# Two more pairs of groups as Strassen pairs in a hybrid decoder layer: the first gate groups and the first output groups

## The chip, the cores and the metric

The kernel runs on one core of one Trainium2 chip. The metric is the device time of one execution in microseconds (us), the median of several runs; lower is better. The profile adds one execution that was recorded by the hardware profiler.

## The reference

One layer of a decoder trunk on 256 tokens with a model width of 2048, all in float32:

```python
h = rmsnorm(x, norm_mix_g)
u = h @ w_in                       # 2048 x 12288
c_g, b_g, xa, za, q, fl, iv, og, ga, gb = split(u)    # eight of 1024 columns, ga and gb of 2048
ya = b_g * causal_dwconv3(c_g * xa, conv_w) * silu(za)
o  = hgrn2_chunked(silu(q), kk(fl), iv, log_f(fl))    # gated linear recurrence, 8 heads of 128
yb = (o / rms(o) * hg_norm_g) * silu(og)
m  = sigmoid(ga) * (ya @ w_a_out) + sigmoid(gb) * (yb @ w_b_out)
x  = x + m @ w_o
x  = x + sigmoid(rmsnorm(x, ple_norm_g) @ w_ple_gate) * (p @ w_ple_proj)
return rmsnorm(x, final_norm_g)
```

## The kernel before

**Groups and steps.** The work is a list of *groups*. A group is a product of the 256 tokens (two row tiles of 128, `t` = 0 and 1) with 512 columns of a weight matrix. It runs over the rows of the weights in *steps* of 256 rows, each a tile of 128 x 1024 (two row tiles of 512 columns). The order is written out: four groups `PP`; for j = 0 and 1 the groups f, q, iv, og, c, xa, za, b; then for j = 0 to 3 the gates ga and gb and the groups A and B (the products with `w_a` and `w_b`, four steps each); then four output groups O with `w_o`, and the groups of `w_pg`. TensorE goes through the steps in this order.

**Precision.** Every float32 operand is split into a rounded high part and the rest, so that a product takes three matmuls: hi x hi, hi x lo, lo x hi. `split(pos)` makes the two parts of a step's weights: an ACTIVATE on ScalarE writes `whi` (L161), a subtraction on VectorE writes `wlo` (L162). A plain step is 2 x 2 x 3 = 12 matmuls of 512 columns.

**Pairs.** Some neighbouring groups run as a *pair* with a program such as

```python
GATES = ("S", 0), (0, 2), ("S", 1), (1, 2), ("S", 4), (0, 6), ("S", 5), (1, 6)
```

An item `(u, c)` stands for two plain steps of group u, from chunk c on; a chunk is 256 rows. An item `("S", c)` is a Strassen unit: chunk c of both groups at once, as a 2 x 2 x 2 block product with seven block products in place of eight, so 21 matmuls where two plain steps take 24. It has four steps, or parts. Its weights have to be combined: `combine_weights` (L176, L179, L180) does three subtractions and additions on VectorE behind the split of part 0; part 1 is a half split of 512 columns (`t2`), parts 2 and 3 are splits of the combined weights. The left operand needs sums of its blocks too: `forms` computes them on VectorE (L761 to L765), and splits them like everything else (on VectorE L769). For h the forms come from a second reading of xT (`forms_of_x`). A pair holds all eight PSUM banks: four of tag g, one for each row tile and group, and four of tag s. `sums` adds the banks up at its end (L810). Before, the pairs are QV and VG (parts of j = 0 and 1), GG for the gates of j = 1, 2 and 3, and GP among the groups of `w_pg`.

**Epilogues.** What follows a group is a generator (`ep_...`), advanced by a yield at every step, so that its instructions stand in the engines' queues between the splits. `turned` turns a tile round: four DMAs to DRAM, one back, and a transpose on VectorE (L332). `ep_bb` multiplies and adds the two branches into a quarter of m, turns it, and splits it into `mh` and `ml` (L889, L890).

**Queues and buffers.** Splits run ahead of their step by `LEAD` = 3 and more. A split needs a buffer: four pairs in pool `wp`, and in some stretches one or two more (`MORE`). The buffer is free when the step that used it before is done. Weights come through three `raw` buffers by SyncE's (SP) DMA queue, which also carries the turning and all else. Each engine takes its instructions in the order of its own queue, which is fixed when the kernel is built.

**Pools.** Two changes of memory pools touch the change: `second_part` closes `tmp1` (with the recurrence's tiles) and opens `m` and `tmp2`, once, after ga of j = 0; `third_part` closes `tmp2` and `branch` and opens `tmp3`, with two steps of the first O group left. Both let all running epilogues finish first.

Of the kernel before, what the change touches and what calls it, by code (L numbers as in the profile page):

```python
# [15 lines left out]
P = 128  # L16
# [25 lines left out]
GATES = ("S", 0), (0, 2), ("S", 1), (1, 2), ("S", 4), (0, 6), ("S", 5), (1, 6)  # L42
INNER = (0, 4), ("S", 0), (0, 6), ("S", 1), (2, 3), ("S", 2), (1, 4), (1, 6)
FRONT = (0, 2), (0, 4), (0, 6), ("S", 0), (1, 2), ("S", 1), (1, 4), (1, 6)
LATE = (0, 4), ("S", 0), (0, 6), ("S", 1), (2, 3), ("S", 2), (1, 4), (1, 6)


# [6 lines left out]
def hybrid_kernel(ctx, tc, xT, x, pT, prm, gfin, masks, w_in, w_a, w_b, w_o, w_pg, w_pp, out):  # L54
# [28 lines left out]
    def nm(s):  # L83
        uid[0] += 1
        return f"{s}_{uid[0]}"
# [17 lines left out]
    half = {}  # L103

    def load(pos):
        w, g, c = stream[pos]
        if unit_of[pos] not in loaded:
            raw = wp.tile([P, 2, 2 * CW], F32, tag="raw", bufs=3, name=nm("raw"))
            loaded[unit_of[pos]] = raw
            if joint[pos]:  # L110
                nc.sync.dma_start(out=raw[:, 0, :], in_=w[g, :, c, :])
                for i in range(2):
                    nc.sync.dma_start(
                        out=raw[:, 1, i * CW : (i + 1) * CW], in_=w[g + 1, :, c, (1 - i) * CW : (2 - i) * CW]
                    )
            elif across[pos]:
                for i in range(2):
                    nc.sync.dma_start(out=raw[:, i, :], in_=w[g + i, :, c, :])
            elif FIRST <= pos < FIRST + 20:
                for i in range(2):  # L120
                    nc.sync.dma_start(out=raw[:, i, :], in_=w[g, :, c + i, :])
            elif pos >= FIRST:
                with ExitStack() as order:
                    if groups[steps[pos][0]][0] == "O":
                        order.enter_context(tc.issue_after(state["sent"]))
                    nc.sync.dma_start(out=raw, in_=w[g, :, c : c + 2, :])
        return loaded[unit_of[pos]]

    def load_first(pos, queues):
# [8 lines left out]
    def split(pos, c0=0, c1=2 * CW):  # L138
        part = part_of[pos]
        src = load(pos)[:, part % 2, :]  # L140
        if joint[pos]:

            src = load(pos)[:, part == 3, :]
            if part == 1:
                src, c1 = half[unit_of[pos]], CW

        pool, n = (pools["late"], 6) if (pos - state.get("late", len(steps))) % 10 < 6 and "late" in state else (wp, 4)
        places = [(pool, n, tag) for tag in ("whi", "wlo")]
        n = len(MORE[more(pos)])
        if pos % (4 + n) < n:  # L150
            places = [(pools[name], 1 + (tag == "X"), tag) for name, tag in MORE[more(pos)][pos % (4 + n)]]
        if pos not in parts:
            parts[pos] = tuple(
                pool.tile([P, 2 * CW], F32R, tag=tag, bufs=n, name=nm("w" + x)) for (pool, n, tag), x in zip(places, ("hi", "lo"))
            )
        hi, lo = parts[pos]
        s = slice(c0, c1)
        with ExitStack() as order:
            for i in (*(state["splits"] if more(pos) == "inner" else ()), *(state["before"].pop() if state.get("before") else ())):
                order.enter_context(tc.issue_after(i))  # L160
            a = nc.scalar.activation(out=hi[:, s], in_=src[:, s], func=AF.Copy)  # L161
            v = nc.vector.tensor_tensor(  # L162
                out=lo[:, s], in0=src[:, s], in1=hi[:, s].bitcast(F32), op=ALU.subtract
            )
        state["splits"] = (a.ins, v.ins)
        if joint[pos] and part == 0:
            combine_weights(pos)

    def combine_weights(pos):

        b = load(pos).rearrange("p i (k c) -> p (i k) c", k=2)
        pool, tag, n = ("tmp2", "t2", 2) if pos in gates else ("tmp3", "t2", 1)
        if more(pos) == "inner":
            pool, tag, n = "tmp1", ("both", "aoff")[unit_of[pos] // 2 % 2], 1
        t2 = half[unit_of[pos]] = pools[pool].tile([P, CW], F32, tag=tag, bufs=n, name=nm("t2"))
        nc.vector.tensor_tensor(  # L176
            out=b[:, 0:4:3, :], in0=b[:, 0:3:2, :], in1=b[:, 3:4, :].to_broadcast([P, 2, CW]), op=ALU.subtract
        )
        nc.vector.tensor_tensor(out=t2, in0=b[:, 2, :], in1=b[:, 0, :], op=ALU.add)  # L179
        nc.vector.tensor_tensor(out=b[:, 1, :], in0=b[:, 1, :], in1=t2, op=ALU.subtract)  # L180
# [3 lines left out]
    for n, (kind, j) in enumerate(IN_ORDER):  # L184
        if (kind, j) in (("q", 0), ("iv", 1)):
            groups.append(("VG", j, w_in, n, "hT", INNER) if j else ("QV", j, w_in, n, "hT", FRONT))
        elif (kind, j) in (("iv", 0), ("og", 1)):
            continue
        elif j == 0 or kind not in ("ga", "gb"):
            groups.append((kind, j, w_in, n, "hT"))  # L190
        elif kind == "ga":
            groups.append(("GG", j, w_in, n, "hT", GATES))
        if kind == "gb":
            groups.append(("A", j, w_a, j, "yaT"))
            groups.append(("B", j, w_b, j, "ybT"))
    groups += [("O", j, w_o, j, "mT") for j in range(4)]
    groups += [("PG", 0, w_pg, 0, "x1T"), ("GP", 1, w_pg, 1, "x1T", LATE), ("PG", 3, w_pg, 3, "x1T")]
    steps = []
    active, done = [], 0
# [8 lines left out]
    for gi, (kind, j, w, g, op, *program) in enumerate(groups):  # L208
# [4 lines left out]
        for n, (u, c) in enumerate(program[0]):  # L213
# [10 lines left out]
    LEAD = 3  # L224
    MORE = {
        None: (), "gates": ((("tmp2", "whi"), ("tmp2", "wlo")),),
        "inner": (
            (("tmp1", "X"), ("tmp1", "X")), (("tmp1", "a"), ("tmp1", "y")),
        ),
    }  # L230
    of_kind = lambda *kinds: [pos for pos, (gi, c) in enumerate(steps) if groups[gi][0] in kinds]
    gates, late = of_kind("GG"), of_kind("PG")[0]
    gates = range(gates[0] - 12, gates[-1] + 9)
    inner = [of_kind(kind) for kind in ("QV", "VG")]
    inner = range(inner[0][0] - 3, inner[0][-1] + 1), range(inner[1][0] - 6, inner[1][-1] + 1)

    def more(pos):

        return "gates" if pos in gates else "inner" if any(pos in at for at in inner) else None

    TOKENS, NORM, FORMS, MASKS = 10, 13, 5, 30
    FIRST = 6
# [552 lines left out]
    def forms_of_x(joined, made):  # L795

        for n in range(0, len(joined), 2):
# [8 lines left out]
            yield from forms("hT", made(n), r, chunks)  # L806
            yield

    def add(out, x, y):
        nc.vector.tensor_tensor(out=out, in0=x, in1=y, op=ALU.add)  # L810

# [45 lines left out]
    def ep_inner(j, e, left):  # L857
# [307 lines left out]
    def third_part():  # L1165
# [7 lines left out]
        xs, state["more"] = whole[:, : NT * D].rearrange("p (t d) -> p t d", t=NT), whole[:, NT * D : NT * D + 1]  # L1173
        state["x"], state["whole"] = xs, whole
        residual(0)
        state["ss2"] = sc(8, "ss2", 1)
        state["ss3"] = sc(12, "ss3", 1)
        nc.gpsimd.memset(state["ss3"].rearrange("p (t j) -> p t j", t=NT)[:, :, 5:6], EPS)
# [11 lines left out]
    def advance():  # L1190
        for e in list(active):
            step(e)
# [78 lines left out]
    for pos, (gi, c) in enumerate(steps[:last_group]):  # L1271
# [43 lines left out]
            step(active[-1])  # L1315
        if pos == MASKS:
            nc.sync.dma_start(out=mask_t, in_=masks)
        if program:
            program = program[0]
            if c == (0, 0):  # L1320
                total = products_of(program)
                left, banks = dict(total), {}
            if c == (min(n for n, (u, _) in enumerate(program) if u == "S"), 0):
# [42 lines left out]
        if c == nch - 1:  # L1366
            if kind == "f" and j == 0:

                waiting = psum
            if kind == "ga" and j == 0:  # L1370
                finish()
                second_part()
                active.append(forms_of_x(sorted(c for u, c in GATES if u == "S"), lambda n: form_tiles(pools["tmp2"], f"Sx{n}")))
                step(active[-1])
            if kind == "O" and j == 0:
                state["x1T"] = operand(big, "x", KT)
            if kind == "f" and j == 0:
                continue
            active.append(epilogues[kind](j, psum))
# [100 lines left out]
```

## Time and profile before

| | us |
|---|---|
| median of 3 runs | 811.68 (811.56 to 811.70) |
| the profiled execution | 810.99 |
| its span, first to last instruction | 809.2 |
| TensorE (PE) busy | 799.4 |
| VectorE (DVE) busy | 657.4 |
| ScalarE (ACT) busy | 474.6 |

The page's row of tenths shows each engine's busy share in 40 slices of the span; a group's row gives line, engine, operation, output and inputs, shape and count, then busy time and the mean of one in ns, then the idle time of the engine before them and what ended it. A window's row gives busy times of PE, PEld (weight load), DVE, ACT and POOL, then the granted clock, the DMA share and GB/s. In the timeline a row has start and length in us. The stages named in the text: the ga and gb groups of j = 0 run from 375.00 to 418.52 us, the first GG pair from 440.28 to 481.08, the O groups from 627.96 on.

### The profile page before, as it was taken

To read this page: it belongs to the slowest core of one execution; us is meant where nothing else is said; L and a number is where in the kernel's file an instruction comes from. 1 tells how busy PE (TensorE), PEld (TensorE's weight loads), DVE (VectorE), ACT (ScalarE), POOL (GpSimd) and SP (SyncE) were. 2 spreads that over 40 slices of the span, in tenths; PEclk is the share of its full clock that TensorE was granted. 3 is DMA by queue.
4 is the path that set the end of the run, shared out by engine and by line. 5 is a ranking of instruction groups with operands and counts; after the bars stand their busy time and mean duration, and the time that the engine had idled before them with its cause. 6 is when DMAs were issued, how large, how long until landed. Compare 5 with 4: busy or idle time off the path is not lost.

```text
span 809.2 us, 11053 instructions
## 1 busy us (share of the span) xinstructions
PE 799.4 (99%) x4183; PEld 665.1 (82%) x4184; DVE 657.4 (81%) x786; ACT 474.6 (59%) x627; POOL 92.1 (11%) x74
## 2 busy tenths in 40 slices
PE   9999999999999999999999999999999999999995
PEld 7888888888888888888888888888888888888885
DVE  5979897967889987967868998998996657679894
ACT  6967565555664765555664564565564456665662
POOL 0000145300000144300001001000100000001032
PEclk9999999999999999999999999999999999999998
DMA  9898856647677654656774774674766687887532
GB/s 342 301 338 312 274 183 207 222 159 247 238 256 228 240 196 170 228 188 228 266 240 151 240 274 146 226 271 150 254 250 217 217 300 262 288 300 272 205 133 105
DMA packets 47862, 188.60 MB, mean 233 GB/s; under 512 B 5440, under 2 KB 14912, under 8 KB 33088
## 3 DMA queue, kind: packets, MB, share of 16 engines
q1 hardware_dynamic: 47664, 187.62, 66.9%
q8 instruction: 33, 0.54, 0.3%
q10 hardware_dynamic: 144, 0.26, 0.1%
q14 instruction: 21, 0.17, 0.1%
HBM read 174.23 MB, written 13.63 MB: 232 GB/s over the span
## 4 chain that ended last, share of the span: by engine, by line
PE 91%; DVE 5%; issue 2%; ACT 1%; DMA 1%; POOL 0%; ACTq 0%; POOLq 0%; DVEq 0%
PE g L1210 62%; PE g L1232 20%; PE s L1232 6%; DVE wlo L162 2%; DMA raw<-in_w_pg 1%; PE s L1210 1%; PE s L482 1%; DVE t L971 1%; PE s L1085 1%; DVE raw L176 0%; DVE t L810 0%; DVE xs L972 0%; DVE t L989 0%; PE s L615 0%; PE s L638 0%
## 5 line engine op out<-in xcount | busy, mean ns | idle before, releaser
L162 DVE TENSOR_TENSOR wlo<-raw,whi 128x1024 fp32r<-128x1024 f32 (+1 forms) x315 | 387.6, 1250 | 119.5 <-ACT whi L161 118.3
L161 ACT ACTIVATE whi<-raw 128x1024 fp32r<-128x1024 f32 (+1 forms) x315 | 323.0, 1048 | 216.0 <-PE g L1210 157.1
L1210 PE MATMUL g<-whi,xh 128*128 128x512 f32 (+1 forms) x528 | 202.3, 384 | 0.0
L1210 PE MATMUL g<-wlo,xh 128*128 128x512 f32 (+1 forms) x528 | 202.1, 383 | 0.0
L1210 PE MATMUL g<-whi,xl 128*128 128x512 f32 (+1 forms) x528 | 201.9, 383 | 0.0
L1210 PEld LDWEIGHTS g<-whi,xl 128*128 128x128 f32 x528 | 99.2, 188 | 19.4
L1210 PEld LDWEIGHTS g<-whi,xh 128*128 128x128 f32 x528 | 99.3, 188 | 19.3
L1210 PEld LDWEIGHTS g<-wlo,xh 128*128 128x128 f32 x528 | 99.3, 188 | 19.2
L1232 PE MATMUL g<-whi,xl 128*128 128x512 f32 x264 | 102.7, 389 | 0.0
L1232 PE MATMUL g<-wlo,xh 128*128 128x512 f32 x264 | 102.7, 389 | 0.0
L1232 PE MATMUL g<-whi,xh 128*128 128x512 f32 x264 | 102.4, 389 | 0.0
L1232 PEld LDWEIGHTS g<-wlo,xh 128*128 128x128 f32 x264 | 49.6, 188 | 10.3
L1232 PEld LDWEIGHTS g<-whi,xl 128*128 128x128 f32 x264 | 49.6, 188 | 10.3
L1232 PEld LDWEIGHTS g<-whi,xh 128*128 128x128 f32 x264 | 49.6, 188 | 10.3
L161 ACT ACTIVATE whi<-t 128x512 fp32r<-128x512 f32 x20 | 12.6, 632 | 70.3 <-DVE t L179 70.3
L1210 PE MATMUL g<-whi,mh 128*128 128x512 f32 x128 | 49.8, 389 | 0.0
L1210 PE MATMUL g<-wlo,mh 128*128 128x512 f32 x128 | 49.8, 389 | 0.0
L1210 PE MATMUL g<-whi,ml 128*128 128x512 f32 x128 | 49.6, 389 | 0.0
L883 POOL TENSOR_TENSOR t<-ga,gb 128x512 f32<-128x512 f32 x6 | 10.6, 1786 | 190.5 <-issue 118.1
L1210 PEld LDWEIGHTS g<-wlo,mh 128*128 128x128 f32 x128 | 24.0, 188 | 5.0
L1210 PEld LDWEIGHTS g<-whi,mh 128*128 128x128 f32 x128 | 24.0, 188 | 5.0
L1210 PEld LDWEIGHTS g<-whi,ml 128*128 128x128 f32 x128 | 24.0, 188 | 4.9
(287 smaller groups left out, 1003.9 us busy)
## 6 DMA issues: line engine op xcount, KB each, us to landing
raw<-in_w_in SPq DMA_DIRECT2D x70, 1024.0 KB, 4.9
raw<-in_w_in SPq DMA_DIRECT2D x35, 512.0 KB, 5.1
raw<-in_w_o SPq DMA_DIRECT2D x16, 1024.0 KB, 5.9
raw<-in_w_pg SPq DMA_DIRECT2D x12, 1024.0 KB, 5.4
turn<-t SPq DMA_DIRECT2D x72, 128.0 KB, 2.6
t<-turn SPq DMA_DIRECT2D x18, 512.0 KB, 4.9
raw<-in_w_in SPq DMA_DIRECT2D x34, 256.0 KB, 4.7
raw<-in_w_a SPq DMA_DIRECT2D x8, 1024.0 KB, 5.2
```

Source lines behind the costliest of these rows:

```text
L161: a = nc.scalar.activation(out=hi[:, s], in_=src[:, s], func=AF.Copy)
L162: v = nc.vector.tensor_tensor(out=lo[:, s], in0=src[:, s], in1=hi[:, s].bitcast(F32), op=ALU.subtract)
L482: nc.tensor.matmul(heads(bk)[r, h, c if at is None else slice(at, at + 32)], key(h)[:, r], query(h)[:, c], start=True, stop=True, tile_pos ...
L883: (nc.vector if j == 3 else nc.gpsimd).tensor_tensor(out=spread(m, t), in0=blocks(ga[:, s]), in1=blocks(gb[:, s]), op=ALU.add)
L971: nc.vector.tensor_tensor(out=gt[:, s], in0=gt[:, s], in1=pw[:, s], op=ALU.mult)
L1085: nc.tensor.matmul(wb[:m, :n], *ones, start=True, stop=True)
L1210: nc.tensor.matmul(psum, a, b, start=first and n == 0, stop=last and n == 2)
L1232: nc.tensor.matmul(banks[name], x, y[:, s], start=k == total[name] and i == 0, stop=k == 1 and i == 2)
```

## The change

The gate groups ga and gb of j = 0 become a pair G0 with the program `GATES`, and the first two O groups a pair OO with a new program `OUT`. Each has four Strassen units. G0's forms of h are made early, in tiles of `tmp1`, by a further reading of xT, and made again in `tmp2` for the later pairs. OO needs forms of m: `ep_bb` stores the first two quarters of m, turned, in DRAM, and `forms_of_m` reads them back during A of j = 3. The change of pools and the start of the pair's epilogue move to G0's last unit (`opening`) and to the last unit of OO. Buffers for splits are added in G0 (from `tmp1`) and in OO (from `yaT`), and in the stretches `tied` each split is held in order behind the one before. The residual of x is loaded for two output groups at once.

```diff
+OUT = ("S", 0), (0, 4), ("S", 1), (1, 4), ("S", 2), (0, 6), ("S", 3), (1, 6)
...
-            for i in (*(state["splits"] if more(pos) == "inner" else ()), *(state["before"].pop() if state.get("before") else ())):
+            for i in (*(state["splits"] if more(pos) == "inner" or any(pos in at for at in tied) else ()), *(state["before"].pop() if state.get("before") else ())):
...
-        elif j == 0 or kind not in ("ga", "gb"):
+        elif kind not in ("ga", "gb"):
             groups.append((kind, j, w_in, n, "hT"))
         elif kind == "ga":
-            groups.append(("GG", j, w_in, n, "hT", GATES))
+            groups.append(("GG" if j else "G0", j, w_in, n, "hT", GATES))
...
-    groups += [("O", j, w_o, j, "mT") for j in range(4)]
+    groups += [("OO", 0, w_o, 0, "mT", OUT), ("O", 2, w_o, 2, "mT"), ("O", 3, w_o, 3, "mT")]
...
+        "last": ((("tmp2", "whi"), ("tmp2", "wlo")), (("branch", "yaTh"), ("branch", "yaTl"))),
+        "first": ((("tmp1", "a"), ("tmp1", "y")), (("tmp1", "b"), ("tmp1", "v"))),
...
-    gates = range(gates[0] - 12, gates[-1] + 9)
+    opening = of_kind("G0")[0] + max(n for n, (u, c) in enumerate(GATES) if u == "S") * 3 + 3
+    g0 = range(of_kind("G0")[0], opening + 1)
+    tied = [range(opening - 21, opening + 12), range(of_kind("OO")[0] - 2, of_kind("OO")[0] + 28)]
+    gates = range(opening + 5, of_kind("OO")[0] + 2)
+    last = range(gates[-1] + 1, gates[-1] + 21)
...
+    def forms_of_m():
+        for j in range(2):
+            raw = t4()
+            nc.sync.dma_start(out=raw, in_=state["m", j])
+            yield
+            yield
+            yield
+            r = raw.rearrange("p (u k t) -> p u k t", u=2, k=2)
+            yield from forms("mT", form_tiles(pools["tmp2"], f"Sx{2 * j}"), r, (2 * j, 2 * j + 1))
...
+    def ep_out(j, e, left):
+        def then(q, g):
+            after = ep_o(j + q, [g[:, A], g[:, B]])
+            next(after)
+            active.append(after)
+        yield from sums(e, left, lambda: (t4(), t4()), then)
...
+        if j < 2:
+            d = state["m", j] = dram.tile([P, 1024], F32, tag="m", bufs=2, name=nm("m"))
+            yield
+            yield
+            nc.sync.dma_start(out=d, in_=m)
...
+        if pos == g0[0] - 9:
+            homes = lambda n: lambda: tuple(
+                pools["tmp1"].tile([P, 1024], F32R, tag=tag, bufs=1 + (tag == "X"), name=nm("form"))
+                for tag in (("kT", "qT") if n else ("X", "X"))
+            )
+            active.append(forms_of_x(sorted(c for u, c in GATES if u == "S"), homes))
+            step(active[-1])
...
+            if kind == "OO" and c == (6, 3):
+                finish()
+                third_part()
+                state["x1T"] = operand(big, "x", KT)
+                active.append(ep_out(j, banks, left))
+                step(active[-1])
+            if pos == opening:
+                finish()
+                second_part()
+                active.append(forms_of_x(sorted(c for u, c in GATES if u == "S"), lambda n: form_tiles(pools["tmp2"], f"Sx{n}")))
+                step(active[-1])
+                active.append(ep_pair(j, banks, left))
+                step(active[-1])
...
-        if kind == "O" and j == 0 and c == nch - 3:
-            finish()
-            third_part()
-        if kind == "O" and j > 0 and c == 1:
+        if kind == "A" and j == 3 and c == 0:
+            active.append(forms_of_m())
+            step(active[-1])
+        if kind == "O" and c == 1:
             residual(j)
```

More of the change, by code (lines that the diff above doesn't have):

```diff
@@ L105, in load, with load_raw @@
     def load(pos):
+        if unit_of[pos] not in loaded and groups[steps[pos][0]][0] in ("O", "OO"):
+            with tc.issue_after(state["sent"]):
+                return load_raw(pos)
+        return load_raw(pos)
+    def load_raw(pos):
         w, g, c = stream[pos]
@@ L122, in load @@
             elif pos >= FIRST:
[L123 to L126, printed above, removed]
+                nc.sync.dma_start(out=raw, in_=w[g, :, c : c + 2, :])
         return loaded[unit_of[pos]]
@@ L153, in split @@
             parts[pos] = tuple(
-                pool.tile([P, 2 * CW], F32R, tag=tag, bufs=n, name=nm("w" + x)) for (pool, n, tag), x in zip(places, ("hi", "lo"))
+                pool.tile([P, 2 * CW << (tag[:3] == "yaT")], F32R, tag=tag, bufs=n, name=nm("w" + x))[:, : 2 * CW] for (pool, n, tag), x in zip(places, ("hi", "lo"))
             )
@@ L171, in combine_weights @@
         b = load(pos).rearrange("p i (k c) -> p (i k) c", k=2)
-        pool, tag, n = ("tmp2", "t2", 2) if pos in gates else ("tmp3", "t2", 1)
-        if more(pos) == "inner":
+        pool, tag, n = ("tmp2", "t2", 2) if more(pos) in ("gates", "last") else ("tmp3", "t2", 1)
+        if more(pos) in ("inner", "first"):
             pool, tag, n = "tmp1", ("both", "aoff")[unit_of[pos] // 2 % 2], 1
@@ L237, in more @@
     def more(pos):
-        return "gates" if pos in gates else "inner" if any(pos in at for at in inner) else None
+        return "gates" if pos in gates else "last" if pos in last else "first" if pos in g0 else "inner" if any(pos in at for at in inner) else None
     TOKENS, NORM, FORMS, MASKS = 10, 13, 5, 30
@@ L1175, in third_part @@
         residual(0)
+        residual(1)
         state["ss2"] = sc(8, "ss2", 1)
@@ L1322, in hybrid_kernel @@
                 left, banks = dict(total), {}
-            if c == (min(n for n, (u, _) in enumerate(program) if u == "S"), 0):
+            if c == (min(n for n, (u, _) in enumerate(program) if u == "S"), 0) and kind not in ("G0", "OO"):
                 active.append({"GG": ep_pair, "GP": ep_gates_late, "QV": ep_inner, "VG": ep_inner}[kind](j, banks, left))
@@ L1369, in hybrid_kernel @@
                 waiting = psum
[L1370 to L1376, printed above, removed]
             if kind == "f" and j == 0:
```

## The prediction

> **What bounds the kernel now.** I read the profile's head first, then the chain that ended last, then single stages.
>
> ```profile
> span 809.2 us, 11053 instructions
> PE 799.4 (99%) x4183; PEld 665.1 (82%) x4184; DVE 657.4 (81%) x786; ACT 474.6 (59%) x627; POOL 92.1 (11%) x74
> PE   9999999999999999999999999999999999999995
> PEclk9999999999999999999999999999999999999998
> PE 91%; DVE 5%; issue 2%; ACT 1%; DMA 1%; POOL 0%; ACTq 0%; POOLq 0%; DVEq 0%
> 80.34 54.40 PE g L1210 x240
> ```
>
> TensorE (PE) is dense from start to end, so a matmul that goes is worth its whole pitch, and a wait of TensorE costs its whole length. The last line, a piece of the chain, gives the pitch: 54.40 us over 240 matmuls is 0.2267 us. The profiled execution took 810.99 us (span 809.2 and 1.8 around it), 0.7 under the median of 811.68; I add differences to the median.
>
> Next, the three stages that matter: the ga group of j=0, the gate pair of j=1 (already in Strassen form), and the first output group. The columns that I use are the window, PE and DVE (VectorE) busy time.
>
> ```profile
> 375.00:396.76 21.76, 21.76 (x98) 18.02 (x97) 18.07 (x28) 11.40 (x14) 0.00 (x0) 1.00 0.85 297
> 440.28:481.08 40.80, 40.80 (x182) 33.79 (x181) 38.53 (x39) 24.61 (x27) 3.53 (x2) 1.00 0.72 246
> 627.96:649.70 21.74, 21.74 (x97) 18.01 (x96) 14.23 (x14) 9.34 (x10) 0.00 (x0) 1.00 0.71 246
> ```
>
> The existing pair keeps VectorE busy 38.53 of 40.80 us with almost nothing in it but its own weights. The ga group, where the change puts a new pair, has 18.07 us of VectorE work in 21.76, and only eight weight splits are among it.
>
> **Matmuls removed.** A plain pair of groups has 8 chunks of 24 matmuls. A Strassen unit does a chunk with 21. Eight units save 24 matmuls: 24 x 0.2267 = 5.44 us. If nothing else moved: 811.68 - 5.44 = 806.2.
>
> **VectorE work added.** Rows for a split (L162), for the combining of weights (L176, L179, L180), and for what else stands in that stage:
>
> ```profile
> L162 DVE TENSOR_TENSOR wlo<-raw,whi 128x1024 fp32r<-128x1024 f32 x17 | 20.7, 1224 | 10.5 <-ACT whi L161 10.5
> L162 DVE TENSOR_TENSOR wlo<-t,whi 128x512 fp32r<-128x512 f32 x20 | 13.8, 691 | 0.9
> L176 DVE TENSOR_TENSOR raw<-raw 128x1024 f32<-128x1024 f32 x3 | 3.7, 1224 | 0.1
> L179 DVE TENSOR_TENSOR t<-raw 128x512 f32<-128x512 f32 x20 | 13.8, 692 | 0.7
> L180 DVE TENSOR_TENSOR raw<-raw,t 128x512 f32<-128x512 f32 x20 | 13.8, 692 | 0.6
> L714 DVE SCALAR_TENSOR_TENSOR cv<-t,prm_t,cv 128x127 f32<-128x127 f32 x16 | 4.9, 345 | 1.2 <-ACT cv L705 1.2
> L714 DVE SCALAR_TENSOR_TENSOR cv<-t,prm_t,cv 128x1 f32<-128x1 f32 x24 | 4.4, 212 | 0.0
> L365 DVE TENSOR_TENSOR t<-g,t 128x512 f32<-128x512 f32 x10 | 6.4, 674 | 0.0
> L332 DVE STREAM_TRANSPOSE t<-t 128x1024 f32<-128x1024 f32 x16 | 19.8, 1238 | 1.0 <-DMA t<-turn 1.0
> L289 DVE SCALAR_TENSOR_TENSOR ybTl<-t,prm_t,ybTh 128x256 fp32r<-128x256 f32 x8 | 3.3, 476 | 0.0
> L735 DVE TENSOR_TENSOR t<-cv,t 128x1024 f32<-128x1024 f32 x2 | 2.4, 1216 | 0.0
> L739 DVE TENSOR_TENSOR yaTl<-t,yaTh 128x1024 fp32r<-128x1024 f32 x2 | 2.4, 1218 | 0.0
> L761 DVE SCALAR_TENSOR_TENSOR t<-t 128x256 f32<-128x256 f32 x1 | 0.4, 427 | 0.2 <-ACT t L785 0.2
> L765 DVE TENSOR_TENSOR t<-t,t 128x256 f32<-128x256 f32 x1 | 0.4, 417 | 0.0
> L769 DVE TENSOR_TENSOR Sx0l<-t,Sx0h 128x1024 fp32r<-128x1024 f32 x1 | 1.2, 1218 | 0.0
> ```
>
> A unit replaces two splits (2.45 us) by three and a half and the combining (3 x 1.224 + 0.691 + 1.224 + 2 x 0.692 = 6.97): 4.5 us more, 36 us over eight. The question is where TensorE is made to wait for it. For that I count VectorE's queue, in the order in which the changed kernel's instructions stand, against TensorE's due times. VectorE takes them strictly in that order here.
>
> ```profile
> 378.77 1.23 DVE L162 TENSOR_TENSOR wlo<-raw,whi 128x1024 fp32r<-128x1024 f32 x1 [0.45 <-ACT whi L161]
> 381.49 1.23 DVE L162 TENSOR_TENSOR wlo<-raw,whi 128x1024 fp32r<-128x1024 f32 x1 [1.49 <-ACT whi L161]
> 450.29 5.77 DVE L162 TENSOR_TENSOR wlo<-raw,whi 128x1024 fp32r<-128x1024 f32 x5 [0.47 <-ACT whi L161]
> 627.24 1.37 DVE L878 TENSOR_TENSOR gb<-gb,g 128x512 f32<-128x512 f32 x2 [2.39 <-PE g L1210]
> 629.73 1.22 DVE L162 TENSOR_TENSOR wlo<-raw,whi 128x1024 fp32r<-128x1024 f32 x1
> 641.82 1.22 DVE L890 TENSOR_TENSOR ml<-t,mh 128x1024 fp32r<-128x1024 f32 x1 [1.13 <-ACT mh L889]
> L161 ACT ACTIVATE whi<-raw 128x1024 fp32r<-128x1024 f32 (+1 forms) x315 | 323.0, 1048 | 216.0 <-PE g L1210 157.1 <-issue 15.5 <-DMA raw<-in_w_in 13.0
> ```
>
> Three things come from here. First, the splits of the ga group start 2.72 us apart, one plain step (12 x 0.2267), and wait for ScalarE, which waits for a buffer: with four buffers the lead of a finished split over its use is 3 x 2.72 - 1.05 - 1.22 = 5.9 us. Second, five splits take 5.77 us: successive starts are (5.77 - 1.22) / 4 = 1.137 apart, 0.087 under the duration. Third, behind a unit's half split VectorE stands 0.47 us, as ScalarE takes the next operand only when L180 has written it.
>
> **The first gate pair.** From its first step up to the first split of its fifth item, (0, 6), stand three units and four plain steps: 63 + 48 = 111 matmuls, 25.2 us. VectorE has in that stretch 13 whole splits (15.9) and 3 half ones (2.1), 3 combinings (7.8), and, left from the recurrence and the convolution of j=1: 8 convolution pieces like the 345 ns row (2.7) and 6 of 212 (1.3), two L365 (1.3), two transposes (2.5), four L289 (1.9), L735 and L739 (2.4), and one set of h's forms, L761 to L765 (4 x 0.42) and L769 (2.9). That is 40.8 us; 45 of them overlap the next by 0.087 (-3.9), and two half splits are followed by the wait of 0.47 (+0.9): 37.8. TensorE then waits 37.8 - 25.2 - 5.9 = 6.7 us. While it waits, buffers come back late too, and VectorE stands behind ScalarE's next eviction, between 0 and one eviction and split (2.3) in all; I take 1.5, as several waits follow each other: 8.2 us. The rest of the pair gains nothing back, since the lost time is TensorE's.
>
> **The output pair.** Here the fixed point is the end of B's last group: the multiplies of m's last quarter wait for it (the 627.24 row), and to the next split from there pass 2.49 us. Behind them stand in the queue, up to the split of the third item's first step: three more splits, then a combining and its half split, the wait of 0.47, two splits, one whole set of forms of m, and the split itself: 2.49 + 3.4 + 2.7 + 0.6 + 0.5 + 2.3 + 2.5 + 1.2 = 15.7 us, against 66 matmuls, 15.0. Then the transpose of m's last quarter (1.15), the wait for ScalarE's copy (1.13, the 641.82 row), its low part (1.13), two splits, a combining, a half split, 0.47 and a split: 26.2 us against 99 matmuls, 22.4. TensorE is 3.8 us late there; I take 4.0 with the buffers. Wider: 2 to 6.
>
> **Sum.** -5.44 + 8.2 + 4.0 = +6.8: 811.68 + 6.8 = 818.5 us.
>
> The 5.77 us row speaks for that overlap. [...]
>
> **Edits that I cost at nothing.** Second reading of xT, and m's first two quarters written and read back:
>
> ```profile
> t<-in_xT SPq DMA_DIRECT2D x13, 256.0 KB, 6.2
> xs<-in_x SPq DMA_DIRECT2D x8, 256.0 KB, 5.2
> raw<-in_w_o SPq DMA_DIRECT2D x16, 1024.0 KB, 5.9
> ```
>
> These are 3 MB more on SP's queue, in stages whose DMA share is 0.71 to 0.85; weights are asked for some steps ahead. If one held a weight load, it would cost up to 5.9 us, less the lead. Above: two evictions of x's residual come together at the end of the output pair, SP waits there for TensorE with a load of w_o behind it; the load is used seven steps (some 18 us) later, and residual plus load take 5.2 + 5.9. Banks: the pair's last sums free O2's two banks about 0.5 us before use; between 0 and 1.5 us, I take 0. ScalarE gains evictions, but is busy 59%. Forms of m wait for data written two groups earlier: 0. The new buffers (tmp1's, yaT's) come when VectorE is the limit, and so bring nothing: 0, or a gain of one more split's lead (1.1 us).
>
> **Rivals.** *VectorE has more lead than I give it.* If the splits entered the first pair some 14 us ahead, TensorE would stay dense, and the time is 806.2; with over 6.8 us of the lateness gone it turns faster. For it: the two new buffer pairs. Against: the 1.49 us idle row shows splits held by buffers up to the pair's first step. 7%.
>
> *Half the lateness.* Buffers and order give 3 us each back: 811 to 814.5. 13%, of which 5 lie within 0.2%.
>
> *TensorE's clock drops.* PEclk is 9 in every slice but the last, where TensorE has stopped and it is 8. If the waits of the first pair let it fall to half, so that 20 matmuls run at half the rate, they lose 20 x 0.2267 = 4.5 us: 823. Against: my longest single wait is 2.7 us, in a stretch that is otherwise busy, and no slice here shows what such a wait does. 6%. [...]
>
> *The change of pools blocks SP or the banks* at the output pair's end: one load, +4 us: 822.5. 4%.
>
> **Numbers.** The forecast has 70% and spans 814.5 to 821.5 (lateness 6.7 to 10.5 in the first pair, 2 to 6 in the second, of which the extremes don't meet). Taking in the nearer half of the smaller lateness and of the two upper cases: 813.5 to 822.5. A difference of 0.2% (1.6 us) is what a measurement can tell. Faster 0.08, same 0.05, slower 0.87.
>
> **What would show it.** PE's count falls by 24 matmuls of 512 columns. Between the first pair's second unit and its fifth item TensorE shows gaps ended by VectorE's wlo, some 8 us, and the windows there show DVE near full; in the output pair some 4 us around m's last quarter. All else stays dense, and the gate pairs of j=1 to 3 keep 40.8 us. I am wrong if the first gate pair takes 41 us (then VectorE had lead), if it takes over 52, if the gaps are ended by DMA, or if PEclk falls.

## The result and the profile after

The changed kernel takes 826.25 us (median of four, 824.92 to 826.8) against 811.69 beside it on the same chip: 1.018 times, interval 1.016 to 1.0195. That is 14.6 us slower. The forecast was 6.8 us slower, with a range that ended at 822.5. The direction and the main mechanism were right, and the size was off by a factor of two.

The profiled execution took 825.77 us (span 824.0). The page first: span, busy time, slices and the chain.

```profile
span 824.0 us, 11170 instructions
PE 805.3 (98%) x4160; PEld 658.9 (80%) x4160; DVE 707.4 (86%) x860; ACT 493.3 (60%) x657; POOL 95.2 (12%) x74
PE   9999999999999999999899999999999999999996
PEclk9999999999999999999999999999999999999999
PE 74%; DVE 14%; ACT 4%; issue 4%; DMA 2%; SPq 0%; POOL 0%; ACTq 0%; POOLq 0%; DVEq 0%
```

VectorE is busy 50.0 us longer than before (707.4 against 657.4), and its share of the chain that ended last rose from 5% to 14%. TensorE still reads 98%: in slices of 20 us, a loss of 15 us in 824 shows as a single 8. So the loss has to be looked for stage by stage. The next windows are five stages of the changed kernel: the gate pair of j=0, the gate pair of j=1, the output pair, what follows it up to the last projections' pair, and the first 34 matmuls behind that, where the groups of `w_pg` begin to mix. The columns are the window, its length, busy time of PE, PEld, DVE, ACT and POOL, the granted clock, the DMA share and GB/s. Windows of pairs, here and below, lie up to 0.8 us off the pair's own first and last matmul, by the same amount at both ends; TensorE is dense there, so their lengths are the pairs'.

```profile
375.45:426.91 51.46, 46.50 (x182) 33.83 (x181) 48.14 (x63) 29.02 (x40) 0.00 (x0) 0.97 0.61 205
448.67:491.72 43.05, 42.08 (x182) 33.43 (x181) 41.71 (x44) 25.09 (x28) 3.53 (x2) 1.00 0.68 230
638.60:684.74 46.14, 43.36 (x182) 32.93 (x181) 43.16 (x48) 24.27 (x27) 0.00 (x0) 1.00 0.61 208
684.74:745.80 61.06, 60.37 (x265) 49.37 (x264) 46.10 (x57) 40.97 (x63) 1.61 (x1) 1.00 0.94 325
745.59:754.07 8.48, 8.12 (x35) 6.23 (x34) 8.41 (x11) 4.94 (x8) 0.00 (x0) 1.00 0.73 257
```

A dense pair of 180 matmuls takes 40.8 us. So TensorE loses 10.7 us in the first gate pair, 2.2 in the second, 5.3 in the output pair, and 1.2 behind it (the same stretch takes 59.84 us in a later kernel without waits). That is 19.4; less the 5.44 saved it is 14.0 of the 14.8 us by which the span grew. The remaining 0.8 is the last window: its 34 matmuls take 7.71 us when dense (34 x 0.2267, and 7.71 in the kernel before), and 8.48 here.

The long wait of the first pair, as VectorE's queue shows it (timeline of the changed kernel: start, length, engine, line, operation):

```profile
392.38 1.22 DVE L166 TENSOR_TENSOR wlo<-raw,whi 128x1024 fp32r<-128x1024 f32 x1
393.52 1.24 DVE L342 STREAM_TRANSPOSE t<-t 128x1024 f32<-128x1024 f32 x1
394.68 0.70 DVE L724 SCALAR_TENSOR_TENSOR cv<-t,prm_t,cv 128x126 f32<-128x126 f32 x3
395.33 0.88 DVE L299 SCALAR_TENSOR_TENSOR ybTl<-t,prm_t,ybTh 128x256 fp32r<-128x256 f32 x2
396.14 0.21 DVE L724 SCALAR_TENSOR_TENSOR cv<-t,prm_t,cv 128x1 f32<-128x1 f32 x1
396.27 1.22 DVE L166 TENSOR_TENSOR wlo<-raw,whi 128x1024 fp32r<-128x1024 f32 x1
```

And TensorE's side of it:

```profile
397.54 0.79 PE L1268 MATMUL g<-wlo,xh 128*128 128x512 f32 x1 [2.45 <-DVE wlo L166]
398.13 0.63 PE L1268 MATMUL g<-whi,xl 128*128 128x512 f32 x1
398.56 0.63 PE L1268 MATMUL g<-wlo,xh 128*128 128x512 f32 x1
...
401.00 0.40 PE L1268 MATMUL g<-wlo,xh 128*128 128x512 f32 x1
```

VectorE runs without a break, but between two splits it has 2.75 us of turning, recurrence and convolution to do, and TensorE has no lead left to cover it. Behind the wait the matmuls stand 0.43 us apart, half the rate, until 401.00.

### The profile page after: what moved, and what is told of

Read it like the earlier page. It is cut to its first block, busy times and chain, and to the rows that moved or that the text cites. A ratio compares the mean times of both kernels' runs of the same rounds, so it can differ in the third digit from the quotient of the medians.

```text
span 824.0 us, 11170 instructions
## 1 busy us (share of the span) xinstructions
PE 805.3 (98%) x4160; PEld 658.9 (80%) x4160; DVE 707.4 (86%) x860; ACT 493.3 (60%) x657; POOL 95.2 (12%) x74
## 4 chain that ended last, share of the span: by engine, by line
PE 74%; DVE 14%; ACT 4%; issue 4%; DMA 2%; SPq 0%; POOL 0%; ACTq 0%; POOLq 0%; DVEq 0%
PE g L1246 43%; PE g L1268 22%; DVE wlo L166 6%; PE s L1268 6%; ACT whi L165 2%; DMA raw<-in_w_pg 2%; DVE raw L180 1%; DVE t L183 1%; DVE t L342 1%; PE s L1246 1%; PE s L492 1%; DMA raw<-in_w_in 1%; PE s L1120 1%; DVE t L1006 0%; DVE raw L184 0%
## 5 line engine op out<-in xcount | busy, mean ns | idle before, releaser
L1246 PE MATMUL g<-whi,xl 128*128 128x512 f32 (+1 forms) x464 | 177.1, 382 | 0.4 <-DVE xl L299 0.4
L1246 PE MATMUL g<-wlo,xh 128*128 128x512 f32 (+1 forms) x464 | 177.3, 382 | 0.0
L1246 PE MATMUL g<-whi,xh 128*128 128x512 f32 (+1 forms) x464 | 177.1, 383 | 0.0
L1268 PE MATMUL g<-wlo,xh 128*128 128x512 f32 x304 | 119.6, 394 | 2.9 <-DVE wlo L166 2.9
L180 DVE TENSOR_TENSOR raw<-raw 128x1024 f32<-128x1024 f32 x28 | 35.2, 1258 | 0.7
L1246 PE MATMUL g<-wlo,yaTh 128*128 128x512 f32 (+1 forms) x74 | 27.9, 383 | 0.0
L1246 PE MATMUL g<-whi,yaTl 128*128 128x512 f32 (+1 forms) x74 | 27.9, 383 | 0.0
L1246 PE MATMUL g<-whi,yaTh 128*128 128x512 f32 (+1 forms) x74 | 27.8, 385 | 0.0
L1246 PE MATMUL g<-wlo,mh 128*128 128x512 f32 x64 | 25.0, 391 | 0.5 <-DVE wlo L166 0.5
L1246 PE MATMUL g<-whi,ml 128*128 128x512 f32 x64 | 24.9, 389 | 0.0
```

Source lines behind the costliest of these rows:

```text
L180: nc.vector.tensor_tensor(out=b[:, 0:4:3, :], in0=b[:, 0:3:2, :], in1=b[:, 3:4, :].to_broadcast([P, 2, CW]), op=ALU.subtract)
L1246: nc.tensor.matmul(psum, a, b, start=first and n == 0, stop=last and n == 2)
L1268: nc.tensor.matmul(banks[name], x, y[:, s], start=k == total[name] and i == 0, stop=k == 1 and i == 2)
```

## The experiments

**Each part alone.** The first kernel leaves the output groups plain, the second leaves the gate groups plain:

```diff
-    groups += [("OO", 0, w_o, 0, "mT", OUT), ("O", 2, w_o, 2, "mT"), ("O", 3, w_o, 3, "mT")]
+    groups += [("O", j, w_o, j, "mT") for j in range(4)]        # gates_only
```
```diff
-        elif kind not in ("ga", "gb"):
+        elif j == 0 or kind not in ("ga", "gb"):                # out_only
```

> Only the gate pair of j=0 is in Strassen form; the output groups stay plain, m is not written or read back. Theory, that VectorE's queue behind a pair's own units makes TensorE wait, each pair by itself: the waits read in the changed kernel were 10.4 us in this pair and 2.2 in the next one (j=1), so 811.7 - 2.7 + 12.6 = 821.6 us, within 0.8. Rival, that the two parts hinder each other through what they share (weight buffers, SP's queue with 3 MB more on it): the parts do not add; this one alone then loses under 8 us, 817 or less.

> Only the first two output groups become a Strassen pair; the gate groups of j=0 stay plain. Theory: the waits read around this pair were 5.1 us in it, 1.2 in output group 3 and 0.7 behind, so 811.7 - 2.7 + 7.0 = 816.0 us, within 0.8, and the stage of the gates is as in the kernel before. Rival (shared things): 814 or less, or waits at other places.

Measured, against 811.23 us: 822.29 us (1.0136, 1.0119 to 1.0153) and 815.57 us (1.0053, 1.0038 to 1.0068). Their losses are 11.1 and 4.3 us, together 15.4 where both have 14.6. Each interval is over 1 us wide to either side, so the parts add, and what they share does not make them hinder each other. What loads and buffers do inside each part, this does not say. The trace of the second kernel also says where the loss in the gate pair of j=1 comes from: without the new gate pair that pair is dense.

```profile
440.21:481.01 40.80, 40.80 (x181) 33.78 (x180) 38.53 (x39) 24.36 (x27) 3.53 (x2) 1.00 0.72 244
```

**The first gate pair without the combining of its weights:**

```diff
     def combine_weights(pos):
+        if pos in g0:
+            half[unit_of[pos]] = b[:, 1, :]
+            return
```

> The changed kernel without the three combining operations of VectorE in the four units of the gate pair of j=0 (that part of the weights' arithmetic is left out; its half split reads the raw weights). VectorE loses 4 x 2.6 = 10.4 us there and everything else stays: loads, buffers, banks, copies of ScalarE. Theory: the waits in this pair, 10.4 us, fall to between 0 and 2, and the time is 826.2 - 8.4 to 10.4 = 815.8 to 817.8 us. Rival, that buffers, banks or loads set these waits: they stay at 8 us or more, 824 to 827.

Measured 818.62 us (1.009, 1.0075 to 1.0105): 7.6 us less (7.2 by the differences to the kernel before), not the 8.4 to 10.4 expected, and far from the rival. The pair and its wait, from the windows and the timeline of that kernel:

```profile
375.11:420.52 45.41, 42.95 (x182) 34.59 (x181) 40.99 (x55) 29.20 (x37) 0.00 (x0) 0.96 0.77 257
...
393.71 0.50 PE L1271 MATMUL g<-wlo,xh 128*128 128x512 f32 x1 [2.46 <-DVE wlo L166]
```

The pair's loss falls from 10.7 to 4.6 us. So the combining makes over half of it; that is shown. The one long wait stays, at 2.46 us: in the 2.8 us ahead of it (390.50 to 393.30) VectorE is busy without a break with the same transpose, convolution and recurrence operations. That these make the rest of the loss is read from the trace, not tried.

**The second gate pair.** Two ideas for its 2.2 us: GpSimd's additions beside the splits, or h's second set of forms, which the change has moved into this pair.

```diff
-            (nc.vector if j == 3 else nc.gpsimd).tensor_tensor(
+            (nc.vector if j in (0, 3) else nc.gpsimd).tensor_tensor(     # m_on_vector
```
```diff
-                active.append(forms_of_x(sorted(c for u, c in GATES if u == "S"), ...))
-                step(active[-1])
+                for n in (0, 2):                                         # forms_at_once
+                    active.append(forms_of_x((2 * n, 2 * n + 1), lambda _, n=n: form_tiles(...)))
+                    step(active[-1])
```

> The changed kernel with the two additions of m of j=0 on VectorE in place of GpSimd. Theory for the 2.2 us of waits in the gate pair of j=1: GpSimd's 3.53 us there stand beside two splits that take 4.23 us together in place of 2.3, and that is what makes VectorE late; VectorE gains 1.4 us of work and loses 1.9 of slowing, but the work comes in front of the forms, so the waits fall by 0.5 to 2.2: 824.0 to 825.7 us. Rival, that the second set of h's forms alone, which now falls into this pair, uses up VectorE's lead: the waits stay or grow by the 1.4 us: 826.2 to 827.6.

> The changed kernel, but the two sets of h's forms for the gate pairs of j=1 to 3 are made side by side, so that the second set's five operations (2.9 us of VectorE) stand ahead of that pair and ahead of the two additions of GpSimd; work and loads are the same. Theory, that this set standing in the pair of j=1 uses up VectorE's lead there: its 2.2 us of waits go, 824.0 us, within 0.6. Rival, that GpSimd's additions beside two splits set these waits: they stay above 1.5 us, 825.4 to 826.6.

Measured 825.66 us (1.0175, 1.016 to 1.0191) and 827.03 us (1.0195, 1.0181 to 1.0209). The first number lies just inside its theory's range, but against the changed kernel's own ratio of 1.0177 it is no difference; the second is at most a slight loss. In their traces the pair of j=1 took 42.63 and 44.88 us, against 43.05: without GpSimd's additions 1.8 of the 2.2 us stay, and with the forms made ahead of the pair it loses more. Neither idea is the cause. What GpSimd's additions (3.53 us, from 451.33 on) do to two splits is real, though (the changed kernel, then the one with the additions on VectorE):

```profile
451.71 4.23 DVE L166 TENSOR_TENSOR wlo<-raw,whi 128x1024 fp32r<-128x1024 f32 x2
```
```profile
453.52 2.35 DVE L166 TENSOR_TENSOR wlo<-raw,whi 128x1024 fp32r<-128x1024 f32 x2
```

The clue lies ahead of the pair, between 418 and 449 us of the changed kernel: ScalarE waits 2.3 us for one load of `w_a`, and VectorE 2.5 us for ScalarE's `whi`. The first gate pair has used up all lead. As I read it, its weight buffers come back late, so the next load lands late, ScalarE and then VectorE stand idle, and the side work (sums of the gates, forms) slides into the pair of j=1. The two-unit kernel below keeps GpSimd's additions and has the forms side by side, as the second kernel here, but no lateness ahead; its pair of j=1 takes 41.15 us, and the kernel without the combining, less late, has 42.24. With the dense pair of the kernel without a new gate pair (above), that fits a loss handed on from the first pair. No run changed this handing on by itself.

**Four units, but late.** If only the sums over the whole pair counted, the units would cost less behind the plain items:

```diff
+TWO = (0, 2), (1, 2), (0, 6), (1, 6), ("S", 0), ("S", 1), ("S", 4), ("S", 5)
-            groups.append(("GG" if j else "G0", j, w_in, n, "hT", GATES))
+            groups.append(("GG" if j else "G0", j, w_in, n, "hT", GATES if j else TWO))
```

> Only the gate pair of j=0, four units, but behind four plain items (and the later forms side by side). Theory (VectorE's work over the whole pair against TensorE's): 32.7 us of the kernel before, less the later pairs' forms 5.8, plus four units 18.0 and their forms 5.8, is 50.6 us against 40.8 and a lead of 5.9: waits 3.9 us, and 1 to 3 more in the next pair from the lead that is missing: 811.2 - 2.7 + 4.9 to 6.9 = 813.4 to 815.4 us. Rival (waits go with the number of units, 2.6 each): 822 us.

Measured 827.58 us (1.0197, 1.0183 to 1.0211), without any output pair: 5 us worse than the four units spread out (the later forms side by side may be up to 1 us of that, as above), and worse than the rival too; 11.7 us of waits lie in the pair, the rest behind it. My sum was wrong, and the trace shows where. First the pair's window, then VectorE over one unit, then TensorE's wait in it:

```profile
376.50:429.02 52.52, 45.44 (x181) 33.96 (x180) 48.90 (x64) 28.33 (x35) 0.00 (x0) 0.97 0.57 191
```
```profile
410.59 1.23 DVE L181 TENSOR_TENSOR raw<-raw 128x1024 f32<-128x1024 f32 x1
411.85 0.69 DVE L184 TENSOR_TENSOR t<-raw 128x512 f32<-128x512 f32 x1
412.58 0.69 DVE L185 TENSOR_TENSOR raw<-raw,t 128x512 f32<-128x512 f32 x1
413.32 0.69 DVE L167 TENSOR_TENSOR wlo<-t,whi 128x512 fp32r<-128x512 f32 x1
414.48 3.50 DVE L167 TENSOR_TENSOR wlo<-raw,whi 128x1024 fp32r<-128x1024 f32 x3 [0.46 <-ACT whi L166]
418.01 1.22 DVE L181 TENSOR_TENSOR raw<-raw 128x1024 f32<-128x1024 f32 x1
...
413.34 0.50 PE L1269 MATMUL s<-whi,form 128*128 128x512 f32 x1 [1.51 <-ACT whi L166]
```

From one unit to the next VectorE takes 418.01 - 410.59 = 7.42 us; TensorE's 21 matmuls take 4.76. Each unit that follows another costs 2.66 us. And little can be saved up for them in the plain items ahead: VectorE is busy 19.25 of the 21.5 us there (376.50 to 398.00). When the first unit was due, at 397.7 us, its first split had been done since 392.1, a lead of 5.7 us. A unit with a plain item of two steps, on the other hand, is 7.42 + 2 x 1.137 = 9.7 us of VectorE for 4.76 + 5.44 = 10.2 us of TensorE. That just fits, if nothing else stands in the queue. This is the measure that the prediction lacked.

This trace also has TensorE's half rate near the pair's end, though no wait ahead of it in the pair is longer than 1.51 us:

```profile
423.00:427.00 4.00, 4.00 (x10) 2.76 (x10) 3.89 (x5) 3.16 (x4) 0.00 (x0) 0.57 0.42 113
```

**Two units, late, each with plain items around it:**

```diff
+TWO = (0, 2), (1, 2), (0, 4), (1, 4), ("S", 0), (0, 6), ("S", 1), (1, 6)     # gates, j=0
-OUT = ("S", 0), (0, 4), ("S", 1), (1, 4), ("S", 2), (0, 6), ("S", 3), (1, 6)
+OUT = (0, 2), (1, 2), (0, 4), (1, 4), ("S", 0), (0, 6), ("S", 1), (1, 6)
```

> Only the gate pair of j=0, with two Strassen units behind four plain items in place of four from its first step on (and the later forms side by side). Theory: what counts is how VectorE's work lies against TensorE's. In the kernel before it is busy 32.7 of 43.5 us in these groups; two units add 9.0, their forms 2.9, and the forms of the later pairs (5.8) move behind: 38.8 of 42.2 us, and the units come when the recurrence is done. Waits 0 to 1 us: 811.2 - 1.4 = 809.8 to 810.8 us. Rival, that each unit costs its share of the 10.4 us wherever it stands (2.6 each): 815 us.

> Only the first two output groups as a pair, with two units behind four plain items; only m's first quarter is written and read back, one set of forms. Theory: VectorE is busy 27.8 of 43.4 us there in the kernel before; two units and one set of forms add 11.9, so 39.7 of 42.1, and m's last quarter is long there when the first unit comes. Waits 0 to 1 us: 809.8 to 810.8 us. Rival, that the waits go with the number of units, half of the 7.0 us: 811.2 - 1.4 + 3.5 = 813.3 us.

> The two pairs together, each with two late units. Theory: the two savings add: 811.2 - 2.7 = 808.5 us, to 810.5 with a wait of 1 us in each. Rival (waits go with the units): 811.2 - 2.7 + 8.7 = 817.2 us.

Measured against 811.47 us: 810.80 (0.9993, 0.9984 to 1.0002), 811.06 (0.9997, 0.9988 to 1.0006) and 811.03 (0.9992, 0.9983 to 1.0): none to be told from no change. The first lies at the upper end of its range, the second 0.3 us and the third 0.5 us above theirs; the rivals, 813 to 817 us, are out. The two pairs in their traces, gates and output:

```profile
376.10:418.26 42.16, 42.16 (x188) 34.91 (x187) 38.61 (x50) 23.85 (x29) 0.00 (x0) 1.00 0.71 244
```
```profile
628.29:670.45 42.16, 42.16 (x187) 34.92 (x186) 33.91 (x36) 19.42 (x22) 0.00 (x0) 1.00 0.68 234
```

In both pairs 186 matmuls run without a gap: 186 x 0.2267 = 42.16 us. The 1.36 us that each should bring are there. Part of them goes elsewhere: in the output kernel behind the pair (below), in the gate kernel not in one place. Its times spread from 809.6 to 811.89.

**The output pair without the combining of its weights** (alone, four units):

```diff
     def combine_weights(pos):
+        if groups[steps[pos][0]][0] == "OO":
+            half[unit_of[pos]] = b[:, 1, :]
+            return
```

> Only the output pair, with four units as changed, but without the combining of its weights (that part of the arithmetic is left out). Theory (VectorE's queue): 10.4 us of work go, and the 5.7 us of waits in the pair fall to 0 to 1; the 1.2 us in output group 3 stay: 809.9 to 811.2 us. Rival, that m's last quarter sets them (its product, transpose through memory, copy and low part must come before any split behind them): at least 3.5 us stay, 813.4 us or more.

Measured 811.98 us against 811.74 (1.0006, 0.9997 to 1.0015): 0.8 us above the theory's range, and 1.4 under the rival's. The pair, from its window:

```profile
628.97:671.61 42.64, 41.44 (x181) 33.56 (x181) 36.35 (x40) 23.73 (x26) 0.00 (x0) 1.00 0.74 252
```

Its loss falls from 5.3 us (in the changed kernel) to 1.8, so two thirds are VectorE's combining. The 1.8 us that stay lie in one place of the trace, at m's last quarter. ScalarE stands 4.00 us until VectorE has turned it, copies it (L921), and takes the next weights only then; TensorE waits for them:

```profile
645.10 1.06 ACT L921 ACTIVATE mh<-t 128x1024 fp32r<-128x1024 f32 x1 [4.00 <-DVE t L344]
646.07 3.46 ACT L165 ACTIVATE whi<-raw 128x1024 fp32r<-128x1024 f32 x4
...
647.16 0.73 PE L1270 MATMUL g<-whi,mh 128*128 128x512 f32 x2 [0.98 <-ACT whi L165]
```

The kernel itself puts these splits behind that copy (`state["before"]`). So the rival names the rest, at half of its 3.5 us or more; no run moved the copy.

**The wait behind the output pair.** In the two-unit output kernel ScalarE had the copies and squares of both epilogues to do, from 696.63 on, ahead of a weight's copy at 701.99, and TensorE stood still:

```profile
696.63 1.71 ACT L951 ACTIVATE t<-t,prm_t 128x256 f32<-128x256 f32 x4 [1.69 <-DVE t L341]
...
704.35 0.50 PE L1245 MATMUL g<-wlo,mh 128*128 128x512 f32 x1 [0.53 <-DVE wlo L166]
```

The epilogues of both output groups run together now. The last experiment starts the second one later, with two units in each pair (as in the third two-unit kernel):

```diff
+        def later(e):
+            for _ in range(4):
+                yield
+            yield from e
         def then(q, g):
             after = ep_o(j + q, [g[:, A], g[:, B]])
+            if q:
+                after = later(after)
```

> Both pairs with two late units each, and the second output group's epilogue starts four steps after the first's. Theory for the 1.2 us of waits in output group 3: the two epilogues run side by side, and ScalarE has 5.3 us of their copies and squares in a row ahead of a weight's copy; apart, the wait goes: 811.0 - 1.2 = 809.8 us. Rival: the waits stay, or turn up behind, in the last projection, 811.0 us or more.

Measured 809.95 us against 811.74 (0.998, 0.9971 to 0.9989): the number that the theory had, and faster than the kernel before, by 1.8 us of the 2.7 that were to be had. Both pairs take 42.16 us again. What follows the output pair, and the 34 matmuls behind that:

```profile
671.51:731.35 59.84, 59.84 (x266) 49.55 (x265) 44.25 (x55) 40.41 (x64) 1.61 (x1) 1.00 0.88 307
730.54:739.24 8.70, 8.31 (x35) 6.22 (x34) 8.63 (x12) 4.91 (x8) 0.00 (x0) 1.00 0.85 307
```

The first stretch is dense now, where the same two pairs without the later start lose 1.2 us. But the second takes 1.0 us more than its dense 7.71, which that kernel has there. So in the profiled executions the wait has moved, as the rival said, and not gone. The medians differ by 1.1 us, but the two ratios' intervals overlap (0.9983 to 1.0 there): that the later start made the kernel faster is not shown.

**The clock.** Six single splits of the kernel before were repeated:

```diff
+        for _ in range({70: 6, 78: 7, 116: 8, 126: 8, 271: 8, 292: 9}.get(pos, 0)):
+            v = nc.vector.tensor_tensor(out=lo[:, s], in0=src[:, s], in1=hi[:, s].bitcast(F32), op=ALU.subtract)
```

> The kernel before, in which six single splits are repeated on VectorE 6 to 9 times (same result) so that TensorE, dense otherwise, waits once each: about 1.2, 2.3, 4.1, 2.9, 3.4 and 4.4 us by lead and count. If a single wait of 2.5 us or more brings the half rate (matmuls 0.43 us apart in place of 0.227, as read behind a wait of 2.45 us), it follows four of the six; if it takes the several shorter waits that came before that one, it follows none. 16 to 18 us more in all, 828 to 835 us.

One run: 865.43 us. The waits were much longer than I meant (other work of VectorE came between the repeats), so the sum says nothing, but single waits can be read. The shortest one and one of 3.10 us:

```profile
194.75 0.50 PE L1214 MATMUL g<-wlo,xh 128*128 128x512 f32 x1 [2.53 <-DVE wlo L166]
195.09 0.40 PE L1214 MATMUL g<-whi,xl 128*128 128x512 f32 x1
...
761.10 0.79 PE L1214 MATMUL g<-wlo,xh 128*128 128x512 f32 x1 [3.10 <-DVE wlo L162]
761.70 0.63 PE L1214 MATMUL g<-whi,xl 128*128 128x512 f32 x1
762.12 0.63 PE L1214 MATMUL g<-wlo,xh 128*128 128x512 f32 x1
```

The half rate (0.43 us from one matmul to the next, seven matmuls) follows behind this wait of 3.10 us, and not behind the one of 2.53 us (0.23 to 0.24 us). By an estimate it stood behind others too: the three groups of 528 matmuls with `xh` and `xl` are busy 615.7 us here and 606.3 in the kernel before, 9.4 us more, and these seven matmuls make 1.8 of it (4.49 us against 7 x 0.383). How many of the six waits it followed, the rows do not show. So a single wait was enough here, as TensorE is dense otherwise, and the second theory, that it takes several, falls; the bound of 2.5 us that I had given the first was a little low for this place. But the half rate also came without so long a wait: the kernel with four late units had it (clock 0.57 from 423.00 to 427.00, above) behind three waits of 1.39 to 1.51 us, 7.5 us apart, and smaller ones between.

## Why the prediction was right in sign and wrong in size

- **TensorE dense, 24 matmuls worth 5.44 us:** right. PE has 23 matmuls less on the page, 4160 against 4183 (a record can be missing: the page before has 4183 matmuls and 4184 weight loads), and where nothing waits the saving shows in full: the two-unit pairs, six matmuls short of 192, take 42.16 us.
- **VectorE's queue makes TensorE wait, in the first gate pair and the output pair:** right; the gaps end with the weights' splits, and without the combining the losses fall from 10.7 to 4.6 and from 5.3 to 1.8 us. Loads, buffers and banks, which I set at nothing, are at most the smaller rest. The overlap that the sum counts held: three splits in a row take 3.50 us in the kernel with four late units, where single ones take 1.22 each.
- **First gate pair, 8.2 us: too small by 2.5.** I let VectorE work from a lead of 5.9 us with breaks of 2.4 us in all: 0.9 behind two half splits and 1.5 behind ScalarE. Three rows at the start of the pair, with idle time in brackets, already have more:

```profile
373.95 0.74 DVE L724 SCALAR_TENSOR_TENSOR cv<-t,prm_t,cv 128x127 f32<-128x127 f32 x3 [0.88 <-ACT cv L715]
375.70 1.22 DVE L166 TENSOR_TENSOR wlo<-raw,whi 128x1024 fp32r<-128x1024 f32 x1 [1.01 <-ACT whi L165]
378.63 2.36 DVE L166 TENSOR_TENSOR wlo<-raw,whi 128x1024 fp32r<-128x1024 f32 x2 [1.70 <-ACT whi L165]
```

  Those are 3.6 us, and with 0.6 behind a later half split 4.2. ScalarE was the one it waited for, and ScalarE was busy with the recurrence's and the forms' operations:

```profile
374.62 1.05 ACT L165 ACTIVATE whi<-raw 128x1024 fp32r<-128x1024 f32 x1
375.57 1.27 ACT L673 ACTIVATE t<-t,rhr 128x128 f32<-128x128 f32 x4
376.75 0.90 ACT L795 ACTIVATE t<-t,prm_t 128x256 f32<-128x256 f32 x2
377.55 3.89 ACT L165 ACTIVATE whi<-raw 128x1024 fp32r<-128x1024 f32 x4
```

  I had set ScalarE aside because it is busy 59% on the whole. That is an average; here it had no gap between 374.62 and 381.44. The step that failed is the term for VectorE's breaks: 4.2 us in place of 2.4, which is 1.8 of the 2.5. The lead at the first step was 5.6 us, not 5.9 (the split was done at 369.6, the first matmul came at 375.2), and VectorE's work in the stretch was some 0.3 us longer. This is read from the trace, not tried.
- **Output pair, 4.0 us: too small by 1.3**, inside my bounds of 2 to 6. I let the multiplies of m's last quarter begin as the pair does, at the end of B. In the trace they begin 1.8 us behind the pair's first matmul (640.14 against 638.35): VectorE still had the low part of a form and two splits to do, without a break. That is enough for the 1.3; it is read from the trace, not tried.
- **"All else stays dense", and 40.8 us for the pairs of j=1 to 3: wrong, by 4.2 us.** This is the larger of the two steps that failed, and the prediction gave no reason for it. The pair of j=1 lost 2.2 us, the groups behind the output pair 1.2, and the start of the last projections 0.8; the pairs of j=2 and 3 did keep 40.8. The first is most likely handed on from the first pair; it comes with that pair, as the kernel without it has none. The second leaves its place when the two epilogues on ScalarE are put apart, but in that trace 1.0 us stands behind it. I had counted the change's cost only inside the new pairs; work that starts later or at the same time is a cost at its new place.
- **The clock:** I called myself wrong if it fell, and it did, in a place that no slice shows:

```profile
397.50:401.00 3.50, 3.46 (x8) 2.75 (x9) 3.47 (x5) 0.00 (x0) 0.00 (x0) 0.52 0.29 54
```

  Some seven matmuls at half rate, 1.4 us by themselves. No run shows the 20 that the rival's 823 us is worked out from. But the seven cost nothing that shows here: in the kernel with the additions on VectorE the same wait of 2.44 us was not followed by the half rate, the clock was 1.00, and the pair took the same time.

```profile
397.82 0.49 PE L1268 MATMUL g<-wlo,xh 128*128 128x512 f32 x1 [2.44 <-DVE wlo L166]
...
406.21 0.50 PE L1268 MATMUL s<-wlo,form 128*128 128x512 f32 x1 [1.10 <-DVE wlo L166]
...
375.11:426.54 51.43, 45.19 (x182) 32.69 (x181) 47.49 (x63) 29.55 (x39) 0.00 (x0) 1.00 0.59 202
```

  51.43 against 51.46 us: TensorE, faster there, only came early to a later weight and waited 1.10 us, where the changed kernel has no wait. With VectorE as the bound, TensorE's rate did not set the time of this pair.
- **The range:** its upper end added bounds inside the two pairs alone. With the 4.2 us of the places that get the moved work it would have reached 826.7, just past the 826.25 measured.

In sum: the span grew by 14.8 us, 8.0 more than the forecast's 6.8 (7.8 by the medians). Of these, 2.5 are VectorE's breaks and lead in the first pair, 1.3 the output pair, and 4.2 the places that I held to be dense.

## What to carry to other kernels

Trading matmuls for elementwise work pays only where the engine that takes the work has time in that very stretch: set the new item with its neighbours against TensorE's time for the same items (here 9.7 us against 10.2 for a unit with a plain item, 7.4 against 4.8 for a unit alone), and count everything else in that queue beyond the lead as a wait. Slack ahead counts only as far as the lead goes (5.7 us in the trace of the late units), so spread the units and put them where nothing else is due. After joining two groups, look also at the places behind: epilogues that now come together, and work that starts later, cost there, and pulling them apart can move the wait one stage on.

## What the hardware showed unexpectedly

- A wait of TensorE of 3.10 us was followed by matmuls 0.43 us apart, in the kernel with repeated splits; one of 2.53 us was not. Waits of 2.44 to 2.46 us at one and the same place went three ways: half rate at once (until 3.46 us after the restart), none, and half rate that began 1.5 us after the restart. In the kernel with four late units it came behind three waits of 1.39 to 1.51 us, 7.5 us apart, and smaller ones between, up to 0.45 us. What decides between these was not shown.
- Two splits of VectorE took 4.23 us beside GpSimd's additions of 3.53 us, and 2.35 us without them. Taking the additions away from GpSimd brought nothing that could be measured (1.0175 times the kernel before, against 1.0177); VectorE then has them to do, in 1.29 us.
